# Two column chunks of an output projection computed as a pair with seven products, and a pinned eviction of the first values

## The chip, the cores and the metric

The kernel runs on one core of a Trainium2 chip (trn2). The metric is the device time of one execution in microseconds (us); three runs of the kernel before took 1334.0 to 1335.42 us, their median is 1334.83 us. One other execution was profiled; it took 1334.18 us, and 1332.5 us of it lie between its first and its last instruction (the span).

## The reference

One decoder layer on 256 rows of width 2048, all in float32, cut to what matters here:

```python
h = rmsnorm(x, g_mix)
proj = h @ w_in                                   # q, k, v of 16 heads and three gates of width 2048
...                                               # three kinds of causal attention: o_a, o_b, o_c
merged = (gates[:, :, 0] * (flat(o_a) @ w_branch[:ea])
          + gates[:, :, 1] * (flat(o_b) @ w_branch[ea:eb])
          + gates[:, :, 2] * (flat(o_c) @ w_branch[eb:]))
x = x + merged @ w_out                            # the output projection, 2048 x 2048
h2 = rmsnorm(x, g_ffn)
gu = h2 @ w_gu                                    # 2048 x 10752 (D_FF = 5376, twice)
x = x + (silu(gu[..., :D_FF]) * gu[..., D_FF:]) @ w_down
```

## The kernel before, in words

**Products.** A float32 matrix is split into a part `hi` that the matmul takes at full speed and a rest `lo`, and each product is three matmuls, `hi*hi`, `hi*lo` and `lo*hi` (L176, L177, L178). Activations stand as columns (k-tiles of 128 by 256 rows) and are the stationary operand, weights stream. A weight tile of two k-tiles by 512 columns (512 KB) is loaded by SP's queue into `w_raw` (4 buffers) or `g_raw` (6 buffers); ScalarE (ACT) casts it to `w_hi` (line 110), VectorE (DVE) subtracts to get `w_lo` (line 110); both have 5 buffers. Such a cast with its subtraction is called a split here. For both halves of the rows (t = 0, 1) one split feeds 12 matmuls of 128x512.

**Plain and paired projections.** `project` computes one column chunk of 512 with 8 splits over the 16 k-tiles, 96 matmuls. `project_pair` computes two chunks at once. For the groups of four k-tiles in `wc` (a list of groups) it forms the 2x2 blocks of rows, k and columns, and takes seven products (`form`, 6 matmuls for each split) of sums of blocks instead of eight: DVE adds weight blocks into tiles `u` (L335, L321), and the activations have sums too (`h_shi`, `h_slo`, from additions at L218 to L221). For the other k-tiles it does plain products (`rest`, 12 matmuls a split). It uses four PSUM tiles, X, Y, Z and V; with `seed` set it copies X to Y and Z to V on ACT, otherwise it takes snapshots. The stages that run so are most of the input projection and the gate-up projection; the output projection runs plainly.

**Rows to columns.** What a projection gives are rows; the next one needs columns. `turn_out` (L718, L720) copies a 128x512 tile as 16-bit halves on ACT and issues a DMA transpose from ACT's queue; `turn_in` (L725) copies it back, and ACT waits in it for the transpose to land. For the merged rows `to_m` places these steps, and the result is `m_hi`, `m_lo`. For the rows after the output projection, `keep_x1` adds the residual (DVE, L1011), squares them on ACT (L438), stores them (L1013), and `next_h` turns column chunks 0 and 1 (in rooms that are `g_raw` buffers); a multiplication by the gain (DVE, L985) follows, then the split to `h_0hi` and so on, then the sums. Chunks 2 and 3 are turned by TensorE (`next_h_now`, L1003).

**Order.** Every engine takes its instructions in program order. A scheduler orders most instructions by its own costs before the launch; those marked `keep_in_program_order` keep their place among themselves. `behind(n, step)` places a step behind the n-th split: the offsets in `to_m` and `next_h` are counted in splits.

**The output projection of before.** Column chunks 0 to 3 follow one another: 12 k-tiles of chunk 0, four of chunk 1, the last four of chunk 0, the rest of chunk 1, then chunks 2 and 3. The k-tiles of the last merged chunk are so needed late. When chunk 3 begins, `begin_pair` starts the weights of the gate-up projection.

**The first values.** `keep_v` hands the eviction of the first value tiles (L803, `v<-ps,rstd`) to the scheduler; rstd is the row norm, finished by GpSimd.

Of the kernel before, what the change touches and what calls it, by code (L numbers as in the profile page):

```python
# [57 lines left out]
def hybrid_block(ctx: ExitStack, tc: tile.TileContext, x, rel_bias, w_in, w_branch, w_out, w_gu, w_down, xT, gains,  # L58
# [29 lines left out]
    pool(ctx, "rim", "right").tile([P, (LINE - 32) // 4], F32, name="rim")  # L88
    wpool = pool(ctx, "wpool", "right", 5)
    scratch = pool(ctx, "scratch", "right", 12)  # L90
    gx = pool(pgx, "gx", "right", 2)

    def half_kb(dt=F32):
# [249 lines left out]
    def project_pair(acts, w, colA, colB, begun=None, nxt=None):  # L343
# [37 lines left out]
        add_into(u, b22)  # L381
        form(X, 6, u, False, True)
        x2 = snapshot(X)
        rest(1, ks[2], Z, V)
        if not by_dma(w, colA):
            add_into(b12, b22)
        form(X, 7, b12, False, True)
        x3 = snapshot(X)
        rest(1, ks[3], Z, V, stop=True)
        if seed:  # L390
            nc.vector.tensor_sub(x3, V, x3)
            c22 = x3
# [28 lines left out]

    p1 = pool(ph1, "p1", "left")
    o_raw = p1.tile([P, NH, S], F32, name="o_raw")
    h = Columns(p1, "h", KT)
    hs = Both(p1, h, WC)

    pa = pool(pat, "pa", "left", 2)

# [369 lines left out]
    def keep_v(g, ps):  # L798
        heads["v", g] = v = pa.tile([P, NT, NB], F32, name="v")

        def scaled():
            for t in range(NT):
                nc.scalar.activation(v[:, t, :], ps[t], AF.Copy, scale=rstd[:, t:t + 1])  # L803
            yield

        if g:
            finish_stages([scaled()])
        else:
            stages.append(scaled())
# [122 lines left out]

    pgx.close()
    m = Columns(pool(pm, "pm", "right"), "m", KT)

    LAST_H = 2

    def to_m(c, srcs, rooms, out_at, in_at):
        n = split_count[0]
        for t in range(NT):  # L940
            behind(n + out_at[t], turn_out, srcs[t], rooms[t])
            behind(n + in_at[t], lambda t: m.put(c, t, turn_in(rooms[t]), True), t)

    def take_gate(gt, src):
        gt.append(half_kb())
# [6 lines left out]
    for c in range(4):  # L952
        turning = [rooms[(NT * c + t) % len(rooms)] for t in range(NT)]
        ms = [room[:, :NB] for room in turning]
        for b, (k0, nk) in enumerate(((0, H_A), (H_A, H_B), (H_A + H_B, H_C))):
            gt = ahead_gates.pop((c, b), None) or list(kept.get((c, b), ()))
            for t in range(NT):
                if (c, b) in unopened:
                    behind(split_count[0] + 1 + t, lambda t, gt: tc.keep_in_program_order(opened(gt[t], gt[t], t)), t, gt)
                elif not gt:  # L960
                    behind(split_count[0] + 1 + t, take_gate, gt, gate_mem[b, c, t])
            if (c, b + 1) in unopened:
                ahead_gates[c, b + 1] = []
                for t in range(NT):
                    behind(split_count[0] + 1 + t, take_gate, ahead_gates[c, b + 1], gate_mem[b + 1, c, t])
            ps = project(o, k0, w_branch, k0 * P, nk, c * NB)
            for t in range(NT):
                if b == 0:
                    nc.vector.tensor_mul(ms[t], ps[t], gt[t])
                else:  # L970
                    nc.vector.tensor_mul(gt[t], ps[t], gt[t])
                    nc.vector.tensor_add(ms[t], ms[t], gt[t])
        if c == unopened[-1][0]:
            tc.keep_in_program_order(nc.scalar.preload_act_table_set("natural_log_exp_and_others"))
        to_m(c, ms, turning, *(((4, 7), (10, 12)) if c < 3 else ((4, 5), (8, 8))))


    def out_of_rows(src, rooms, pl, name, bufs):
# [8 lines left out]

    def next_h(c, xc):
        n, rooms = split_count[0], []
        out_at, in_at = ((4, 8), (11, 14)) if c < 1 else ((4, 7), (9, 11))  # L990
        for t in range(NT):
            behind(n + out_at[t], lambda t: out_of_rows(xc[t], rooms, gx, "g_raw", 6), t)
            behind(n + in_at[t], into_h, c, t, rooms)
        if c in WC:
            behind(n + in_at[1] + 1, lambda: h2.put_sums(c, *[r[:, NB:].rearrange("p (k q) -> p k q", k=4) for r in rooms]))
# [21 lines left out]
        else:  # L1017
            stages.append(next_h_now(c, xc))

    for c in range(4):  # L1020
        xc = [half_kb() for _ in range(NT)]
        for t in range(NT):
            behind(split_count[0] + (1, 2)[t], lambda t: fetch(xc[t], x[t * P:(t + 1) * P, c * NB:(c + 1) * NB]), t)
        if c == 0:
            ps = project(m, 0, w_out, 0, KT, 0, upto=12)
            second = project(m, 0, w_out, 0, KT, NB, upto=4)
            project(m, 0, w_out, 0, KT, 0, ps, 12)
        elif c == 1:
            ps = project(m, 0, w_out, 0, KT, NB, second, 4)
        else:  # L1030
            ps = project(m, 0, w_out, 0, KT, c * NB)
        if c == 0:
            ph1.close()
            pe = pool(ctx, "pe", "left")
            WD = (4, 6, 8)
            ORDER = [0, 1, 2, 4, 3, 6, 5, 8, 7, 9, 10]
            EARLY = 3
            a = Chunks(None, "a", NF // 4, WD, False)
            for e in ORDER[:EARLY]:
                a.place(pe, e)  # L1040
            h2 = Chunks(pool(h2_stack, "h2p", "left"), "h", KT // 4, WC)
            gx = pool(h2_stack, "gx2", "left", 2)
        if c == 3:
            ahead = begin_pair(h2, w_gu, 0, D_FF)
        keep_x1(c, ps, xc)
# [239 lines left out]
```

## Time and profile before

| | before |
|---|---|
| time, median of 3 runs | 1334.83 us (1334.0 to 1335.42) |
| profiled execution | 1334.18 us, span 1332.5 us |
| PE busy | 1325.1 us, 99% |
| DVE busy | 1198.2 us, 90% |
| ACT busy | 939.8 us, 71% |
| GpSimd busy | 61.8 us, 5% |
| input projection and gates | 4 to 540 us |
| branch projection | 540 to 595.4 us |
| output projection | 595.4 to 679.2 us, 384 matmuls |
| gate-up, then down projection | from 679.2 us |

Time outside the span is 1334.18 - 1332.5 = 1.7 us. In the rows of the trace that follow, the first number is the start in us from the span's begin, the second the duration; a `[... <-...]` at the end is idle time of that engine before the row, and what ended it. PE is TensorE, ACTq the queue of ScalarE that issues DMAs. A `x2` sums two rows. Durations of matmuls overlap: the pitch from start to start is what a matmul costs.

### The profile page before, as it was taken

What the parts mean: (1) busy time and instruction counts of PE and PEld (TensorE: products, weight loads), DVE (VectorE), ACT (ScalarE), POOL (GpSimd) and SP (SyncE); (2) the same over time, 40 slices, a digit from 0 to 9 for tenths busy, and PEclk for the clock granted to TensorE, in tenths of its full rate; (3) what the DMA queues carried; (4) which work ended last, traced back from release to release, by engine and by line L of the source; (5) the groups of instructions that cost most, each with busy time, mean ns of one, the idle gap of its engine ahead of it and who ended that gap; (6) DMA issues with size and microseconds to landing.
All of it is one profiled execution on the core that took longest, in us unless ns stands there. A gap on an engine that the chain in (4) does not pass through costs nothing.

```text
span 1332.5 us, 17482 instructions
## 1 busy us (share of the span) xinstructions
PE 1325.1 (99%) x6202; PEld 1152.8 (87%) x6202; DVE 1198.2 (90%) x1261; ACT 939.8 (71%) x1209; POOL 61.8 (5%) x85
## 2 busy tenths in 40 slices
PE   9999999999999999999999999999999999999998
PEld 7888888888888888888888888888888888888887
DVE  7898998999889988785899999999999998999998
ACT  7677867777677766766766778787777776664563
POOL 0300100000111000000020000000000000000000
PEclk9999999999999999999999999999999999999999
DMA  9995868767777866997996966677878887867662
GB/s 342 305 303 173 249 189 258 242 209 229 238 244 246 282 194 239 283 277 230 293 289 234 244 226 234 201 230 256 261 246 221 232 280 255 291 236 275 231 213 102
DMA packets 203623, 325.80 MB, mean 245 GB/s; under 512 B 44648, under 2 KB 55424, under 8 KB 203536
## 3 DMA queue, kind: packets, MB, share of 16 engines
q1 hardware_dynamic: 151488, 291.02, 64.3%
q0 software_dynamic: 8416, 18.44, 6.7%
q10 hardware_dynamic: 43632, 15.24, 5.8%
q8 instruction: 48, 0.79, 0.2%
q14 instruction: 39, 0.32, 0.1%
HBM read 304.18 MB, written 12.08 MB: 237 GB/s over the span
## 4 chain that ended last, share of the span: by engine, by line
PE 87%; DVE 5%; DMA 3%; issue 2%; ACT 2%; POOL 0%; SPq 0%; DVEq 0%; ACTq 0%; POOLq 0%
PE ps L177 11%; PE ps L176 11%; PE ps L178 11%; PE qs L177 10%; PE qs L176 10%; PE qs L178 10%; PE z L177 4%; PE z L178 4%; PE z L176 4%; DVE w_lo L110 3%; PE v L176 2%; PE v L177 2%; PE v L178 2%; ACT w_hi L110 1%; DMA w_raw<-in_w_down 1%
## 5 line engine op out<-in xcount | busy, mean ns | idle before, releaser
L110 DVE TENSOR_TENSOR w_lo<-w_raw,w_hi 128x1024 fp32r<-128x1024 f32 x308 | 373.8, 1219 | 64.9 <-ACT w_hi L110 63.7
L110 ACT CAST w_hi<-w_raw 128x1024 fp32r<-128x1024 f32 x308 | 319.7, 1046 | 75.5 <-PE qs L178 21.5
L110 ACT CAST w_hi<-u 128x1024 fp32r<-128x1024 f32 x156 | 163.2, 1047 | 166.0 <-DVE u L321 87.5
L110 DVE TENSOR_TENSOR w_lo<-g_raw,w_hi 128x1024 fp32r<-128x1024 f32 x208 | 248.0, 1218 | 19.2 <-ACT w_hi L110 17.9
L110 ACT CAST w_hi<-g_raw 128x1024 fp32r<-128x1024 f32 x208 | 214.1, 1048 | 67.8 <-PE ps L178 15.4
L110 DVE TENSOR_TENSOR w_lo<-u,w_hi 128x1024 fp32r<-128x1024 f32 x156 | 186.9, 1219 | 22.0 <-ACT w_hi L110 21.6
L177 PE MATMUL ps<-w_lo,h_hi 128*128 128x512 f32 x328 | 125.0, 381 | 0.5 <-DVE w_lo L110 0.5
L178 PE MATMUL ps<-w_hi,h_lo 128*128 128x512 f32 x328 | 124.3, 379 | 0.0
L177 PE MATMUL qs<-w_lo,h_hi 128*128 128x512 f32 x316 | 120.6, 382 | 0.0
L178 PE MATMUL qs<-w_hi,h_lo 128*128 128x512 f32 x316 | 119.8, 379 | 0.0
L176 PE MATMUL ps<-w_hi,h_hi 128*128 128x512 f32 x328 | 118.6, 381 | 0.1
L176 PE MATMUL qs<-w_hi,h_hi 128*128 128x512 f32 x316 | 114.4, 382 | 0.0
L321 DVE TENSOR_TENSOR u<-u,g_raw 128x1024 f32<-128x1024 f32 x88 | 103.9, 1216 | 0.0
L177 PEld LDWEIGHTS ps<-w_lo,h_hi 128*128 128x128 f32 x328 | 62.0, 189 | 9.5 <-DVE w_lo L110 0.9
L176 PEld LDWEIGHTS ps<-w_hi,h_hi 128*128 128x128 f32 x328 | 61.7, 189 | 9.5 <-ACT w_hi L110 0.7
L178 PEld LDWEIGHTS ps<-w_hi,h_lo 128*128 128x128 f32 x328 | 62.0, 189 | 8.6
L178 PEld LDWEIGHTS qs<-w_hi,h_lo 128*128 128x128 f32 x316 | 59.7, 189 | 8.3
L176 PEld LDWEIGHTS qs<-w_hi,h_hi 128*128 128x128 f32 x316 | 59.5, 189 | 8.5 <-issue 0.4
L177 PEld LDWEIGHTS qs<-w_lo,h_hi 128*128 128x128 f32 x316 | 59.8, 189 | 8.1
L335 DVE TENSOR_TENSOR u<-g_raw 128x1024 f32<-128x1024 f32 x44 | 53.5, 1216 | 1.0 <-DMA g_raw<-in_w_gu 1.0
L176 PE MATMUL v<-w_hi,h_hi 128*128 128x512 f32 x112 | 43.1, 385 | 0.0
L177 PE MATMUL v<-w_lo,h_hi 128*128 128x512 f32 x112 | 42.6, 380 | 0.0
(426 smaller groups left out, 2947.6 us busy)
## 6 DMA issues: line engine op xcount, KB each, us to landing
w_raw<-in_w_in SPq DMA_DIRECT2D x100, 512.0 KB, 5.7
g_raw<-in_w_in SPq DMA_DIRECT2D x88, 512.0 KB, 5.7
g_raw<-in_w_gu SPq DMA_DIRECT2D x88, 512.0 KB, 5.8
w_raw<-in_w_gu SPq DMA_DIRECT2D x88, 512.0 KB, 5.9
w_raw<-in_w_down SPq DMA_DIRECT2D x56, 512.0 KB, 5.1
w_raw<-in_w_branch SPq DMA_DIRECT2D x32, 512.0 KB, 5.2
w_raw<-in_w_out SPq DMA_DIRECT2D x32, 512.0 KB, 5.9
g_raw<-in_w_down SPq DMA_DIRECT2D x32, 512.0 KB, 5.5
```

Source lines behind the costliest of these rows:

```text
L110: for op in nc.scalar.copy(hi, src), nc.vector.tensor_sub(lo, src, hi.bitcast(F32)):
L176: nc.tensor.matmul(ps, ah, wh, start=start, stop=False, **how)
L177: nc.tensor.matmul(ps, ah, wl, start=False, stop=False, **how)
L178: nc.tensor.matmul(ps, al, wh, start=False, stop=stop, **how)
L321: tc.keep_in_program_order(nc.vector.tensor_add(d, d, a))
L335: nc.vector.tensor_add(d, a, b)
```

## The change

1. Chunks 0 and 1 of the output projection run as one `project_pair` with `wc=(0,)`: the first four k-tiles by the seven products, the other twelve plainly, seeded. 19 splits take the place of 16. Its first splits (`begin_pair`) stand ahead of the end of the branch projection. The merged rows of chunk 0 get their sums (`m_sums`); `rest` stands in two loops in the middle.
2. The residual rows of both chunks are loaded together, and `keep_x1` for both comes after the whole pair; `next_h` for chunk 0 gets offsets (1,3),(6,8) in place of (4,8),(11,14). `to_m` for chunk 3 gets (3,4) in place of (4,5).
3. `h` and `hs` move to a pool on the other side of memory, which is freed before the pair's tiles are made.
4. The evictions in `keep_v` are pinned in program order, and the first ones wait until the paired stages have begun.

```diff
+    ph = pool(pgx, "ph", "right")
...
-        rest(1, ks[2], Z, V)
+        middle = ks[2:1 + len(ks) // 2]
+        for k in middle:
+            rest(1, k, Z, V)
...
-        rest(1, ks[3], Z, V, stop=True)
+        for k in ks[2 + len(middle):]:
+            rest(1, k, Z, V, stop=k == ks[-1])
...
         def scaled():
+            while not in_pairs[0]:
+                yield
             for t in range(NT):
-                nc.scalar.activation(v[:, t, :], ps[t], AF.Copy, scale=rstd[:, t:t + 1])
+                tc.keep_in_program_order(nc.scalar.activation(v[:, t, :], ps[t], AF.Copy, scale=rstd[:, t:t + 1]))
...
+    m_sums = Both(pool(pair_stack, "ms", "right"), m, (0,))
+    gx = pool(pair_stack, "gx3", "right", 2)
...
+        if c in m_sums.wc:
+            behind(n + in_at[1] + 1, lambda: m_sums.put_sums(c, *words))
...
+            if (c, b) == (3, 2):
+                ahead = begin_pair(m_sums, w_out, 0, NB, True)
...
-        to_m(c, ms, turning, *(((4, 7), (10, 12)) if c < 3 else ((4, 5), (8, 8))))
+        to_m(c, ms, turning, *(((4, 7), (10, 12)) if c < 3 else ((3, 4), (8, 8))))
...
-        out_at, in_at = ((4, 8), (11, 14)) if c < 1 else ((4, 7), (9, 11))
+        out_at, in_at = ((1, 3), (6, 8)) if c < 1 else ((4, 7), (9, 11))
...
-    for c in range(4):
...
-        if c == 0:
-            ps = project(m, 0, w_out, 0, KT, 0, upto=12)
-            second = project(m, 0, w_out, 0, KT, NB, upto=4)
-            project(m, 0, w_out, 0, KT, 0, ps, 12)
-        elif c == 1:
-            ps = project(m, 0, w_out, 0, KT, NB, second, 4)
-        else:
-            ps = project(m, 0, w_out, 0, KT, c * NB)
...
+    xc = take_x((0, 1), 6)
+    ps, _ = project_pair(m_sums, w_out, 0, NB, ahead)
...
+    for c in range(2):
+        keep_x1(c, ps[NT * c:NT * (c + 1)], xc[c])
+    for c in range(2, 4):
+        xc, = take_x((c,), 1)
+        ps = project(m, 0, w_out, 0, KT, c * NB)
```

What the change does to the order shows at three places. Line numbers shift by a few: L110 is L111 after, L438 is L442, L718, L720 and L725 are L722, L724 and L729, L803 is L809, L985 is L1002, L1011 is L1028, L1013 is L1030.

ScalarE near 40 us, at the end of the first values, before:

```order
L110 CAST w_hi_540<-w_raw_538 128x1024
L803 ACTIVATE v_459<-ps_137,rstd_108 128x512
L803 ACTIVATE v_459<-ps_138,rstd_108 128x512
L110 CAST w_hi_564<-g_raw_556 128x1024
L110 CAST b_shi1_102<-o_raw_97 128x1024
L110 CAST w_hi_568<-g_raw_558 128x1024
L110 CAST w_hi_582<-g_raw_578 128x1024
```

and after:

```order
L111 CAST w_hi_541<-w_raw_539 128x1024
L111 CAST w_hi_565<-g_raw_557 128x1024
L111 CAST b_shi1_105<-o_raw_100 128x1024
L111 CAST w_hi_569<-g_raw_559 128x1024
L809 ACTIVATE v_462<-ps_140,rstd_111 128x512
L809 ACTIVATE v_462<-ps_141,rstd_111 128x512
L111 CAST w_hi_585<-g_raw_581 128x1024
```

Three casts (the first two of the next weights and one of activation sums) moved ahead of the two evictions.

ScalarE at the start of the output projection, where the last merged chunk is turned (`o_raw` is the memory of its rooms), before:

```order
L718 COPY o_raw_97<-o_raw_97 128x1024
L110 CAST w_hi_5641<-w_raw_5639 128x1024
L718 COPY o_raw_97<-o_raw_97 128x1024
L720 DMA_TRANSPOSE o_raw_97<-o_raw_97 128x8x128
L110 CAST w_hi_5661<-w_raw_5659 128x1024
L720 DMA_TRANSPOSE o_raw_97<-o_raw_97 128x8x128
L110 CAST w_hi_5679<-w_raw_5677 128x1024
L725 COPY o_raw_97<-o_raw_97 128x2x512
L110 CAST m_hi_4825<-o_raw_97 128x4x128
```

and after, where `qs_5576` is X, `qs_5577` is Y, `z_5578` is Z and `v_5579` is V of the pair:

```order
L369 COPY qs_5577<-qs_5576 128x512
L722 COPY o_raw_100<-o_raw_100 128x1024
L371 COPY v_5579<-z_5578 128x512
L724 DMA_TRANSPOSE o_raw_100<-o_raw_100 128x8x128
L111 CAST w_hi_5648<-u_5556 128x1024
L722 COPY o_raw_100<-o_raw_100 128x1024
L111 CAST w_hi_5664<-w_raw_5662 128x1024
L111 CAST w_hi_5682<-w_raw_5680 128x1024
L724 DMA_TRANSPOSE o_raw_100<-o_raw_100 128x8x128
L317 COPY sc_5660<-qs_5576 128x512
```

The seed copy of Z to V stands behind the first copy of the merged rows, and casts and a snapshot stand between the transposes and the copies back.

ScalarE behind the end of chunk 0, before, from the first transpose of its new rows to the first copy back:

```order
L720 DMA_TRANSPOSE g_raw_5841<-g_raw_5841 128x8x128
L110 CAST w_hi_5905<-w_raw_5903 128x1024
L110 CAST w_hi_5924<-w_raw_5922 128x1024
L718 COPY g_raw_5928<-sc_5534 128x1024
L720 DMA_TRANSPOSE g_raw_5928<-g_raw_5928 128x8x128
L110 CAST w_hi_5946<-w_raw_5944 128x1024
L1013 DMA x1_93<-sc_5534 128x512
L110 CAST w_hi_5965<-w_raw_5963 128x1024
L110 CAST w_hi_5986<-w_raw_5984 128x1024
L725 COPY g_raw_5841<-g_raw_5841 128x2x512
```

and after, behind the end of the pair (`sc_5572` to `sc_5574` are rows of both chunks):

```order
L722 COPY g_raw_5947<-sc_5572 128x1024
L722 COPY g_raw_5988<-sc_5573 128x1024
L722 COPY g_raw_6009<-sc_5574 128x1024
L111 CAST w_hi_6044<-w_raw_6042 128x1024
L1030 DMA x1_96<-sc_5572 128x512
L724 DMA_TRANSPOSE g_raw_5947<-g_raw_5947 128x8x128
L724 DMA_TRANSPOSE g_raw_5988<-g_raw_5988 128x8x128
L724 DMA_TRANSPOSE g_raw_6009<-g_raw_6009 128x8x128
L729 COPY g_raw_5947<-g_raw_5947 128x2x512
L111 CAST w_hi_6068<-w_raw_6066 128x1024
L722 COPY g_raw_6072<-sc_5575 128x1024
L111 CAST w_hi_6089<-w_raw_6087 128x1024
```

Five casts stood between the first transpose and the copy that waits for it; now three transposes stand in a row and the copy back follows at once. VectorE has the last of the four gain rows, and what follows it, before:

```order
L985 TENSOR_TENSOR g_raw_5969<-g_raw_5969,par_73 128x512
L110 TENSOR_TENSOR h_slo0_5753<-g_raw_5841,h_shi0_5752 128x4x128
L1011 TENSOR_TENSOR sc_5899<-qs_5901,sc_5899 128x512
L110 TENSOR_TENSOR w_lo_6172<-w_raw_6169,w_hi_6171 128x1024
L1011 TENSOR_TENSOR sc_5900<-qs_5902,sc_5900 128x512
```

and after:

```order
L111 TENSOR_TENSOR w_lo_6240<-w_raw_6237,w_hi_6239 128x1024
L111 TENSOR_TENSOR h_slo0_5907<-g_raw_5988,h_shi0_5906 128x4x128
L219 TENSOR_TENSOR g_raw_6072<-g_raw_6072 128x256
L1002 TENSOR_TENSOR g_raw_6009<-g_raw_6009,par_73 128x512
L222 TENSOR_TENSOR g_raw_5947<-g_raw_5947 128x256
L111 TENSOR_TENSOR w_lo_6258<-w_raw_6255,w_hi_6257 128x1024
L220 TENSOR_TENSOR g_raw_6072<-g_raw_6009,g_raw_6072 128x256
L1020 TENSOR_TENSOR sc_6170<-tr_6165,par_73 128x512
L111 TENSOR_TENSOR w_lo_6277<-w_raw_6274,w_hi_6276 128x1024
```

Before, the last gain row stood ahead of the new rows of chunk 2 (L1011, `sc_5899`); it now stands behind them (L1028 in the numbers of after) and ahead of the first rows of chunk 2 that TensorE turned (L1020).

More of the change, by code (lines that the diff above doesn't have):

```diff
@@ L423, in hybrid_block @@
     o_raw = p1.tile([P, NH, S], F32, name="o_raw")
-    h = Columns(p1, "h", KT)
-    hs = Both(p1, h, WC)
+    h = Columns(ph, "h", KT)
+    hs = Both(ph, h, WC)
     pa = pool(pat, "pa", "left", 2)
@@ L934, in hybrid_block, with into_m @@
     m = Columns(pool(pm, "pm", "right"), "m", KT)
+    pair_stack = ExitStack()
+    m_sums = Both(pool(pair_stack, "ms", "right"), m, (0,))
+    gx = pool(pair_stack, "gx3", "right", 2)
     LAST_H = 2
+    def into_m(c, t, room, words):
+        words.append(turn_in(room))
+        m.put(c, t, words[-1], True)
     def to_m(c, srcs, rooms, out_at, in_at):
-        n = split_count[0]
+        n, words = split_count[0], []
         for t in range(NT):
             behind(n + out_at[t], turn_out, srcs[t], rooms[t])
-            behind(n + in_at[t], lambda t: m.put(c, t, turn_in(rooms[t]), True), t)
+            behind(n + in_at[t], into_m, c, t, rooms[t], words)
+        if c in m_sums.wc:
+            behind(n + in_at[1] + 1, lambda: m_sums.put_sums(c, *words))
     def take_gate(gt, src):
@@ L1018, in keep_x1, with take_x @@
             stages.append(next_h_now(c, xc))
-    for c in range(4):
-        xc = [half_kb() for _ in range(NT)]
-        for t in range(NT):
-            behind(split_count[0] + (1, 2)[t], lambda t: fetch(xc[t], x[t * P:(t + 1) * P, c * NB:(c + 1) * NB]), t)
-        if c == 0:
-            ps = project(m, 0, w_out, 0, KT, 0, upto=12)
-            second = project(m, 0, w_out, 0, KT, NB, upto=4)
-            project(m, 0, w_out, 0, KT, 0, ps, 12)
-        elif c == 1:
-            ps = project(m, 0, w_out, 0, KT, NB, second, 4)
-        else:
-            ps = project(m, 0, w_out, 0, KT, c * NB)
[L1032 to L1042, printed above, removed]
+    def take_x(cs, at):
+        xc = [[half_kb() for _ in range(NT)] for c in cs]
+        for i, c in enumerate(cs):
+            for t in range(NT):
+                behind(split_count[0] + at + NT * i + t,
+                       lambda i, c, t: fetch(xc[i][t], x[t * P:(t + 1) * P, c * NB:(c + 1) * NB]), i, c, t)
+        return xc
+    xc = take_x((0, 1), 6)
+    ps, _ = project_pair(m_sums, w_out, 0, NB, ahead)
+    pair_stack.close()
+    ph1.close()
+    pe = pool(ctx, "pe", "left")
+    WD = (4, 6, 8)
+    ORDER = [0, 1, 2, 4, 3, 6, 5, 8, 7, 9, 10]
+    EARLY = 3
+    a = Chunks(None, "a", NF // 4, WD, False)
+    for e in ORDER[:EARLY]:
+        a.place(pe, e)
+    h2 = Chunks(pool(h2_stack, "h2p", "left"), "h", KT // 4, WC)
+    gx = pool(h2_stack, "gx2", "left", 2)
+    for c in range(2):
[3 more added lines that the diff above has]
+        ps = project(m, 0, w_out, 0, KT, c * NB)
         if c == 3:
```

## The prediction

> **What bounds the kernel now.** I read the busy shares first, then the windows around the changed stage, then what TensorE (PE) waits for, and last the timelines of ACT and DVE at the places where the change puts other instructions.
>
> ```profile
> span 1332.5 us, 17482 instructions
> PE 1325.1 (99%) x6202; PEld 1152.8 (87%) x6202; DVE 1198.2 (90%) x1261; ACT 939.8 (71%) x1209; POOL 61.8 (5%) x85
> ...
> L177 PE MATMUL ps<-w_lo,h_hi 128*128 128x512 f32 x328 | 125.0, 381 | 0.5 <-DVE w_lo L110 0.5
> ```
>
> PE leaves 1332.5 - 1325.1 = 7.4 us of the span. The reader should see two bounds in that: no change in the order alone can gain more than some 7 us, and whatever PE waits for that it did not wait for before is paid in full. The next engine is DVE, and how close it is depends on the stage:
>
> ```profile
> core 0: us, PE busy (x) PEld busy (x) DVE busy (x) ACT busy (x) POOL busy (x), PEclk, DMA share, GB/s
> 500.00:600.00 100.00, 100.00 (x465) 87.57 (x464) 79.55 (x92) 67.38 (x71) 0.00 (x0) 1.00 0.88 267
> 600.00:650.00 50.00, 50.00 (x233) 43.78 (x232) 29.73 (x30) 34.37 (x43) 0.00 (x0) 1.00 0.90 268
> 650.00:700.00 50.00, 50.00 (x241) 43.82 (x240) 46.59 (x58) 35.72 (x49) 7.82 (x11) 1.00 0.86 273
> 700.00:800.00 100.00, 100.00 (x465) 87.44 (x464) 95.86 (x92) 71.34 (x80) 0.00 (x0) 1.00 0.75 234
> 800.00:900.00 100.00, 99.97 (x462) 86.59 (x461) 97.19 (x92) 77.81 (x88) 0.00 (x0) 1.00 0.70 223
> ```
>
> In the output projection's first part DVE has 40% to spare, in its second 7%, and in the gate-up stage behind it 3 to 4%. So DVE enters the gate-up stage with whatever lead it has, and cannot win back a lost one there: a delay at 680 us reaches the end of the kernel. PE's waits as such are tiny:
>
> ```profile
> PE ps L177 <- DVE w_lo L110: 0.7, 2, 0.5
> PE z L177 <- DVE w_lo L110: 0.5, 1, 0.5
> ```
>
> **The six matmuls.** The two chunks took 2 x 96 = 192 matmuls; the pair takes 7 products x 6 + 12 rests x 12 = 186. The pitch is 100 us / 465 = 0.215 us (first window), though a row shows 0.38. PE is never idle in this stage, so they lie on the path: -1.29 us.
>
> The Trainium skill, "TensorE: Matmul & The Clock Gate", section "Back-to-back issue gap", gives about 131 ns as the sustained pitch of a 512-column matmul in a stream with weight loads, and 216 ns for one alone. By the first figure the six would save 0.79 us; this trace shows the second in a full stream, so -1.29 stays.
>
> **The pinned first values.** Here PE's longest hole in the stage is visible:
>
> ```profile
> 42.72 1.27 ACT L803 ACTIVATE v<-ps,rstd 128x512 f32<-128x512 f32 x2 [2.18 <-POOL rstd L192]
> ...
> 44.95 1.22 DVE L110 TENSOR_TENSOR w_lo<-g_raw,w_hi 128x1024 fp32r<-128x1024 f32 x1 [3.15 <-ACT w_hi L110]
> ...
> 51.50 0.38 PE L176 MATMUL ps<-w_hi,h_hi 128*128 128x512 f32 x1
> 52.36 0.48 PE L177 MATMUL ps<-w_lo,h_hi 128*128 128x512 f32 x1 [0.48 <-DVE w_lo L110]
> ```
>
> ACT waits 2.18 us for rstd with casts queued behind it, DVE waits 3.15 us for the cast, and PE comes to a w_lo that is late: 52.36 - 51.50 = 0.86 against a pitch of 0.215, a hole of 0.65 us. After, three casts stand ahead of the evictions, and the 2.18 us are filled. I take the whole hole, -0.65 us. The bounds: 0, if the next split is late instead, to -0.65. The later evictions of values (inside the paired stages) are pinned too, so one may hold a PSUM tile longer; in the order it sits behind two copies that PE's transposes release, and the tile is wanted about a microsecond after. I take 0 for it, with a bound of +1.5 (two evictions by 0.64, from the row of 1.27 x2).
>
> **Inside the pair.** DVE gets four weight additions and three more subtractions of 128x1024, 7 x 1.22 = 8.5 us by the 44.95 row, and some smaller sums; in 600 to 650 it was idle 50 - 29.7 = 20 us, and I cost them at 0 under that cover; if the cover is gone, up to 8.5 us of w_lo work is late. ACT gets three casts and some copies, with 15.6 us idle in the same window: 0 by amount. SP loads the same 32 tiles, only in another order: 0. By order ACT is not at 0:
>
> ```profile
> 52.23 0.58 ACT L316 COPY sc<-ps 128x512 f32<-128x512 f32 x1
> ...
> 599.05 1.04 ACT L718 COPY o_raw<-o_raw 128x1024 uint16<-128x1024 uint16 x1 [0.83 <-DVE o_raw L972]
> ...
> 602.02 1.25 ACTq L720 DMA_TRANSPOSE o_raw<-o_raw  x1
> ...
> 606.11 1.34 ACT L725 COPY o_raw<-o_raw 128x1024 uint16<-128x1024 uint16 x1 [1.70 <-DMA o_raw<-o_raw]
> ...
> 609.82 1.35 ACT L725 COPY o_raw<-o_raw 128x1024 uint16<-128x1024 uint16 x1 [1.72 <-DMA o_raw<-o_raw]
> ...
> 611.98 0.61 ACT L110 CAST m_hi<-o_raw 128x512 fp32r<-128x512 f32 x1
> 612.50 2.94 ACT L110 CAST w_hi<-w_raw 128x1024 fp32r<-128x1024 f32 x3
> ...
> 621.30 0.38 PE L176 MATMUL ps<-w_hi,m_hi 128*128 128x512 f32 x1
> ```
>
> The merged rows of the last chunk come at 599.05, 3.6 us after the branch projection's end; their first copy (1.04) now stands ahead of the copy of Z to V (0.58), so V would be ready 3.6 + 0.95 + 0.6 = 5.1 us into the pair; in the new order one weight subtraction of DVE that stood ahead of these rows is gone from there (about 1 us), so 4.2. PE wants it after three forms of 1.29 us, at 3.9: a wait of 0.3 to 0.4. Two issues (602.02) with 1.25 us each follow. Then the last merged columns: before, their cast ended at 612.6 and PE used them first at 621.30, 8.7 us to spare. The pair has no such detour by chunk 1 and wants them about 7 us earlier, and a snapshot now stands ahead of the copy back: I expect two waits of some 0.25 us. Sum of the pair's own waits: +0.9 us, the nearest rows being the 0.5 us waits above. Bounds: 0, and 3, the time between the two copies back (609.82 - 606.11 = 3.7) less what I have counted, if the second transpose is late in full.
>
> **Behind the pair.** This is the large term. Both chunks' residual rows now come at the pair's end, E, where before chunk 0's came 13.5 us ahead of chunk 1's (623.23 and 636.68, L1011). What follows on ACT is priced by these rows:
>
> ```profile
> g_raw<-in_w_gu SPq DMA_DIRECT2D x88, 512.0 KB, 5.8
> ...
> o_raw<-o_raw ACTq DMA_TRANSPOSE x6, 7.9
> g_raw<-g_raw ACTq DMA_TRANSPOSE x6, 6.2
> ...
> 623.23 1.28 DVE L1011 TENSOR_TENSOR sc<-qs,sc 128x512 f32<-128x512 f32 x2
> ...
> 623.94 0.63 ACT L438 ACTIVATE sc<-sc 128x512 f32<-128x512 f32 x1 [0.63 <-DVE sc L1011]
> ...
> 624.58 1.03 ACT L718 COPY g_raw<-sc 128x1024 uint16<-128x1024 uint16 x1
> ...
> 636.68 1.28 DVE L1011 TENSOR_TENSOR sc<-ps,sc 128x512 f32<-128x512 f32 x2
> ...
> 640.40 0.33 ACTq L1013 DMA_DIRECT2D x<-sc  x1
> ...
> 644.86 1.25 ACTq L720 DMA_TRANSPOSE g_raw<-g_raw  x1
> ...
> 646.20 1.05 ACT L110 CAST w_hi<-w_raw 128x1024 fp32r<-128x1024 f32 x1 [1.37 <-issue]
> ...
> 656.66 0.69 DVE L985 TENSOR_TENSOR g_raw<-g_raw,par 128x512 f32<-128x512 f32 x1 [0.44 <-ACT g_raw L725]
> ...
> 671.70 2.47 DVE L335 TENSOR_TENSOR u<-g_raw 128x1024 f32<-128x1024 f32 x2 [0.99 <-DMA g_raw<-in_w_gu]
> 674.08 3.49 DVE L110 TENSOR_TENSOR w_lo<-g_raw,w_hi 128x1024 fp32r<-128x1024 f32 x3
> ...
> 682.65 1.23 DVE L110 TENSOR_TENSOR w_lo<-u,w_hi 128x1024 fp32r<-128x1024 f32 x1 [0.77 <-ACT w_hi L110]
> ...
> 686.64 0.46 PE L177 MATMUL z<-w_lo,h_shi 128*128 128x512 f32 x1
> ```
>
> A DMA transpose holds ACT for 1.25 us while it issues (the cast at 646.20 waited 1.37 for "issue"). From E: additions 1.2, four squares 4 x 0.64 (624.58 - 623.94), three copies and a cast 4 x 0.95 (the pitch (2.94 - 1.04) / 2 of the casts at 612.50), a store 0.33: the first transpose issues at E + 7.8, and three of them hold ACT to E + 11.5. The first lands after 6.2 (median of six), at E + 14.0; ACT sits in the copy back until then, where before five casts stood between the two. The copy costs 1.2 (from 609.82 to the next row). Three casts, a copy, the second copy back, a small cast and two stores (6.2 us) come before the fourth transpose: E + 21.5, landed E + 27.7, copied by E + 29. Two casts, two small casts and a store (3.05) stand before the last copy back (1.2): the last gain row on DVE comes at about E + 33. Before, it came at 656.66 - 636.68 = E + 20.
>
> From that row to the subtraction of the second `u` split of the gate-up weights, the new order has 26 DVE instructions: 11 of 128x1024 at a pitch of 1.135 (row 674.08: (3.49 - 1.22) / 2), 11 of 128x512 at 0.60 (row 636.68: 1.28 - 0.68), 4 of 128x256 at an estimated 0.33, half of that and a little: 20.4 us, ending at E + 53.5. The gate-up weights also wait for rooms: `g_raw` buffers hold the turned rows until DVE's sums are made, then 5.8 us of load and 1 of cast follow. Two such rooms come free 5.5 and 4.3 us of DVE work ahead of the row that needs the new weights: 6.85 - 5.5 and 6.85 - 4.3 less the 1.4 already waited make 1.4 + 1.1 = 2.5 us, or 0 if loads come sooner; the 0.99 at 671.70 is such a wait. PE wants that split after the 192 matmuls of chunks 2 and 3 (41.4), 24 of the gate-up stage (5.2), eight small transposes (0.9) and 7 matmuls (1.5): E + 49.0. Late by 4.5 to 7.0; I take 6.0. Before, the split ended at 683.9 and was used at 686.64, 2.7 us to spare, so this stage held no stall. The lower bound is 0 (the first rival), the upper 7.0 + 2 x 1.7 = 10.4 (the 7.9 of the merged rows' transposes in place of 6.2, in the two rounds that are in series).
>
> **Sum.** -1.29 - 0.65 + 0.9 + 6.0 = +5.0 us on the profiled execution's 1334.18, that is 1339.2. The median of the runs stands 0.65 above that execution, so 1339.8; I say 1340.
>
> **Rivals.**
> - *The rows are hidden anyway.* The lead decides it: DVE may run up to five splits ahead (five `w_lo` buffers), and the wait for E + 14 gives it time to. Had it 4 splits in hand at E + 33 that stand behind this row in the order, 4 x 1.135 = 4.5 us of the 20.4 would be done, and the split is in time. For it: DVE idles 20 us of 600 to 650. Against it: the order is fixed, and the rows of the list stand behind the gain row. It turns at a lateness under 0.5 us; then -1.94 + 0.9 = -1.0, or 1333.8, no slower than before.
> - *Everything in time and the small holes gone.* Also without the pair's waits: -1.94, and up to 0.8 from waits like those of 0.5 above that shift: 1334.83 - 2.7 = 1332.1. Against it: three events must coincide.
> - *The transposes queue behind each other.* Three issue in 3.75 us. If each lands only after the one before (two issued 1.9 us apart in the merged rows were copied back 3.7 apart, 606.11 and 609.82), the last row comes 3 to 5 us later still: 1343 to 1346.
> - *A cold PE.* The granted clock is 1.00 in every window above because PE never stops. A single wait as long as 6 us would be the first of its length; if the clock then halved for as long as the wait lasted, PE would do 3 us of work in those 6, and 3 us are added: 1343. More likely the wait is in five pieces of 1 to 2 us, one at each split. The Trainium skill, "TensorE: Matmul & The Clock Gate", section "HAM oscillation - how this bites in real kernels", warns of idle gaps over about 3.4 us; no run here shows one yet.
>
> **Chances.** Late rows near the sum 0.50, transposes queueing 0.10, cold clock 0.04, hidden 0.28, all gone 0.08. The changes within 0.2% of before (2.7 us, about what a measurement of this kernel can tell from no change) are the hidden rows: 0.28. Faster 0.08, slower 0.64. The likeliest case alone spans 1336 to 1344 (lateness 2 to 10); the range reaches down to the hidden rows, 1333, and up to the queueing transposes, 1346.
>
> **What would show it.** After, PE should have a new group of waits on `w_lo` (L111) near 680 us, in `ps` and `z` rows, of 4 to 7 us in all; ACT a long wait in the copy back (L729) on the transpose some 8 to 14 us behind the pair's end; DVE its last gain row (L1002) about 33 us behind that end; the 0.48 wait at 52 us should be gone. If PE shows no wait at 680 us, the lead was larger than my walk has it, and the prediction is wrong there; if the waits sit in the pair (V, m_hi), its +0.9 was too small.

## The result, and the profile after

The changed kernel is slower: its four runs took 1341.71 to 1349.9 us, median 1344.55, against a median of 1334.65 us before (four runs, 1334.0 to 1335.42). The ratio is 1.008, with a 95% interval of 1.0061 to 1.0099. The profiled execution took 1342.05 us, 7.9 us more than that of before; the rest of the 9.9 us between the medians differs from execution to execution, and is taken up below.

The page of the changed kernel, its first lines:

```profile
span 1340.3 us, 17488 instructions
PE 1328.1 (99%) x6196; PEld 1152.4 (86%) x6196; DVE 1209.8 (90%) x1276; ACT 946.3 (71%) x1218; POOL 63.5 (5%) x85
```

The six matmuls are gone (6202 to 6196) and the share of PE still reads 99%. What PE waits for tells more. Columns: engine, tile and line, what released it, us in total, times, longest:

```profile
PE ps L177 <- ACT w_hi L111: 2.6, 1, 2.6
PE qs L177 <- ACT qs L369: 1.6, 1, 1.6
PE tr L422 <- PEq L1286: 0.8, 1, 0.8
PE ps L178 <- DVE w_lo L111: 0.8, 1, 0.8
PE v L177 <- ACT v L371: 0.5, 1, 0.5
```

The `tr` wait was there before. The other four are new, two in the pair (L369, L371) and two at the start of the gate-up stage. By the starts of PE's rows, before and after:

| stage on PE | before | after | difference |
|---|---|---|---|
| up to the end of the branch projection | 595.40 | 595.08 | -0.3 |
| chunks 0 and 1 of the output projection | to 636.84: 41.4 | to 638.53: 43.4 | +2.0 |
| chunks 2 and 3 | to 679.16: 42.3 | to 681.31: 42.8 | +0.5 |
| gate-up, up to the first V product | to 687.80: 8.6 | to 695.57: 14.3 | +5.6 |
| the rest of the span | 644.7 | 644.7 | 0.0 |

The sum is +7.8 us, the difference of the spans. The pair should have saved 1.3 and cost 2.0, so 3.3 us are lost inside it. The rows of the two largest holes, ScalarE first, then PE, from the timeline of the changed kernel:

```profile
577.79 1.26 ACTq L724 DMA_TRANSPOSE o_raw<-o_raw  x1
...
581.76 4.13 ACTq L724 DMA_TRANSPOSE o_raw<-o_raw  x1
...
592.16 1.35 ACT L729 COPY o_raw<-o_raw 128x1024 uint16<-128x1024 uint16 x1 [3.28 <-DMA o_raw<-o_raw]
...
595.98 1.36 ACT L729 COPY o_raw<-o_raw 128x1024 uint16<-128x1024 uint16 x1
597.37 0.62 ACT L111 CAST m_hi<-o_raw 128x512 fp32r<-128x512 f32 x1
597.89 1.04 ACT L111 CAST w_hi<-w_raw 128x1024 fp32r<-128x1024 f32 x1
598.84 0.58 ACT L369 COPY qs<-qs 128x512 f32<-128x512 f32 x1
...
597.45 0.38 PE L179 MATMUL z<-w_hi,b_slo 128*128 128x512 f32 x1
599.47 0.48 PE L177 MATMUL qs<-w_hi,m_hi 128*128 128x512 f32 x1 [1.64 <-ACT qs L369]
...
601.52 0.48 PE L177 MATMUL v<-w_hi,m_hi 128*128 128x512 f32 x1 [0.48 <-ACT v L371]
```

Read it backwards. PE's second product waits at 599.47 for Y, the copy of X (L369), which starts at 598.84 only. Ahead of it in ScalarE's queue stand the two copies back of merged chunk 2 (592.16 and 595.98), with casts of columns and weights. In the first of them ScalarE waits 3.28 us: its DMA transpose was issued at 577.79 and landed 14.3 us later. The transpose of the second was issued at 581.76 and landed 14.2 us later, at 595.96, just as ScalarE came to it. The two transposes of this chunk took 4.8 and 11.1 us before. V then comes 0.65 us late as well. The holes are 2.02 - 0.22 = 1.8 us and 0.65 us (start to start, less the pitch). Most of the rest of the 3.3 us are holes of 0.1 to 0.2 us: two right behind these, and six from 615.9 to 618.5 us, 0.6 us in all, where the last merged columns are first used.

Behind the pair, ScalarE, VectorE and PE of the changed kernel:

```profile
644.24 1.34 ACTq L724 DMA_TRANSPOSE g_raw<-g_raw  x1
...
650.93 1.35 ACT L729 COPY g_raw<-g_raw 128x1024 uint16<-128x1024 uint16 x1 [3.88 <-DMA g_raw<-g_raw]
...
667.97 0.69 DVE L1002 TENSOR_TENSOR g_raw<-g_raw,par 128x512 f32<-128x512 f32 x1
...
678.33 1.22 DVE L111 TENSOR_TENSOR w_lo<-g_raw,w_hi 128x1024 fp32r<-128x1024 f32 x1
...
681.27 1.05 ACT L111 CAST w_hi<-g_raw 128x1024 fp32r<-128x1024 f32 x1 [5.92 <-DMA g_raw<-in_w_gu]
...
686.89 1.04 ACT L111 CAST w_hi<-g_raw 128x1024 fp32r<-128x1024 f32 x1 [4.05 <-DMA g_raw<-in_w_gu]
...
687.97 1.22 DVE L111 TENSOR_TENSOR w_lo<-g_raw,w_hi 128x1024 fp32r<-128x1024 f32 x1 [3.79 <-ACT w_hi L111]
...
690.31 2.44 DVE L111 TENSOR_TENSOR w_lo<-u,w_hi 128x1024 fp32r<-128x1024 f32 x2
...
687.99 0.48 PE L177 MATMUL ps<-w_hi,h_0hi 128*128 128x512 f32 x1 [2.63 <-ACT w_hi L111]
689.25 0.48 PE L178 MATMUL ps<-w_lo,h_0hi 128*128 128x512 f32 x1 [0.78 <-DVE w_lo L111]
...
692.99 0.63 PE L179 MATMUL z<-w_hi,h_slo 128*128 128x512 f32 x1
693.41 0.60 PE L177 MATMUL z<-w_hi,h_shi 128*128 128x512 f32 x1
```

The last gain row comes at 667.97, the weights of the gate-up stage behind it. ScalarE waits 4.05 us for the sixth `g_raw` load of that stage; it was issued at 679.57, right behind the subtraction at 678.33, which read the buffer that it fills, and landed at 686.80. PE waits 2.63 us for the cast, then 0.78 for its `w_lo`; VectorE stands idle 3.79 us for the same cast. The last two rows show something else: a pitch of 0.42 us, twice 0.215. The granted clock tells why:

```profile
650.00:675.00 25.00, 24.86 (x119) 21.46 (x118) 21.57 (x31) 23.00 (x30) 0.00 (x0) 1.00 0.97 307
675.00:700.00 25.00, 21.47 (x93) 17.75 (x93) 20.27 (x24) 12.09 (x20) 7.25 (x9) 0.93 0.93 273
700.00:725.00 25.00, 25.00 (x117) 21.91 (x116) 24.57 (x25) 17.88 (x20) 0.39 (x2) 1.00 0.70 243
```

In 675 to 700 us the clock is 0.93 of full speed. It falls behind the two waits; that they cause it is tried below (the filled wait). In the 5.6 us of this stage, 2.8 + 1.04 = 3.8 are waits; most of the 1.8 left is the slower pitch. VectorE runs at 98% (24.57 of 25) behind it, and nothing is won back: the rest of the span is as long as before.

### The profile page after: what moved, and what is told of

It reads as the page before. It is cut to its first block, busy times and chain, and to the rows that moved or that the text cites. A ratio compares the mean times of both kernels' runs of the same rounds, so it can differ in the third digit from the quotient of the medians.

```text
span 1340.3 us, 17488 instructions
## 1 busy us (share of the span) xinstructions
PE 1328.1 (99%) x6196; PEld 1152.4 (86%) x6196; DVE 1209.8 (90%) x1276; ACT 946.3 (71%) x1218; POOL 63.5 (5%) x85
## 4 chain that ended last, share of the span: by engine, by line
PE 89%; DMA 4%; DVE 3%; ACT 2%; issue 2%; SPq 0%; ACTq 0%; DVEq 0%
PE ps L178 11%; PE ps L177 11%; PE ps L179 11%; PE qs L177 10%; PE qs L178 10%; PE qs L179 10%; PE z L178 4%; PE z L179 4%; PE z L177 4%; PE v L177 3%; PE v L178 3%; PE v L179 3%; DVE w_lo L111 1%; PE tr L178 1%; PE tr L177 1%
## 5 line engine op out<-in xcount | busy, mean ns | idle before, releaser
L111 DVE TENSOR_TENSOR w_lo<-w_raw,w_hi 128x1024 fp32r<-128x1024 f32 x304 | 369.4, 1221 | 48.8 <-ACT w_hi L111 47.6
L111 ACT CAST w_hi<-w_raw 128x1024 fp32r<-128x1024 f32 x304 | 315.3, 1047 | 61.8 <-PE ps L179 15.4
L111 ACT CAST w_hi<-u 128x1024 fp32r<-128x1024 f32 x159 | 166.1, 1048 | 168.0 <-DVE u L322 90.3
L111 DVE TENSOR_TENSOR w_lo<-g_raw,w_hi 128x1024 fp32r<-128x1024 f32 x212 | 253.2, 1221 | 22.3 <-ACT w_hi L111 21.0
L111 ACT CAST w_hi<-g_raw 128x1024 fp32r<-128x1024 f32 x212 | 218.7, 1049 | 75.3 <-PE ps L179 15.0
L111 DVE TENSOR_TENSOR w_lo<-u,w_hi 128x1024 fp32r<-128x1024 f32 x159 | 191.0, 1221 | 22.4 <-ACT w_hi L111 21.9
L178 PE MATMUL ps<-w_lo,h_hi 128*128 128x512 f32 x344 | 131.1, 381 | 0.0
L179 PE MATMUL ps<-w_hi,h_lo 128*128 128x512 f32 x344 | 130.4, 379 | 0.0
L177 PE MATMUL ps<-w_hi,h_hi 128*128 128x512 f32 x344 | 124.0, 381 | 0.1
L178 PE MATMUL qs<-w_lo,h_hi 128*128 128x512 f32 x300 | 114.7, 382 | 0.0
L179 PE MATMUL qs<-w_hi,h_lo 128*128 128x512 f32 x300 | 113.8, 379 | 0.0
L177 PE MATMUL qs<-w_hi,h_hi 128*128 128x512 f32 x300 | 109.3, 382 | 0.2 <-ACT sc L317 0.2
```

The lines of the kernel that those rows point to most:

```text
L111: for op in nc.scalar.copy(hi, src), nc.vector.tensor_sub(lo, src, hi.bitcast(F32)):
L177: nc.tensor.matmul(ps, ah, wh, start=start, stop=False, **how)
L178: nc.tensor.matmul(ps, ah, wl, start=False, stop=False, **how)
L179: nc.tensor.matmul(ps, al, wh, start=False, stop=stop, **how)
```

## The experiments

**The pin alone.** The kernel before, with the edit of `keep_v` only:

```diff
         def scaled():
+            while not in_pairs[0]:
+                yield
             for t in range(NT):
-                nc.scalar.activation(...)
+                tc.keep_in_program_order(nc.scalar.activation(...))
```

> The kernel before with the pinned evictions of the values alone; the output projection stays plain. If the hole at 51.5 us (0.65 us) is closed and no other opens, the time falls by 0.3 to 0.7 us, 1334.0 to 1334.4 against 1334.65. If the pin holds a PSUM tile in the paired stages, as the bound of +1.5 had it, it is 1335 to 1336. Either way the pair is then answerable for all of the 7 to 10 us that the change costs.

Median 1334.52 us of 11 runs against 1334.37 of 15, ratio 1.000 (0.9991 to 1.0008). In the trace the hole at 51.5 us is gone and the span is 1332.0 against 1332.5, but a new one of 0.3 us stands at 312 us. The gain, if there is one, lies under what the runs resolve; a cost does not show either.

**The pair without the pin.** The same edit taken back in the changed kernel.

> The changed kernel with the evictions of the values left to the scheduler, as before. If the pair alone costs the time, it is 0.3 to 0.7 us slower than the changed kernel in a run with the same clock: 1342.4 to 1343 at best, with the same waits of 2.4 us in the pair and 3 to 4 us at the start of the gate-up stage. If the pin has a part in it, it is more than 1 us faster than the changed kernel.

Median 1345.73 us (1342.37 to 1347.86), ratio 1.008 (1.006 to 1.01), as with the pin. The pair alone is the cause. This kernel's profiled execution was one of the long ones (span 1346.2), and shows what those are made of:

```profile
PE qs L177 <- ACT qs L369: 3.7, 1, 3.7
PE ps L177 <- ACT w_hi L111: 3.6, 1, 3.6
```

```profile
600.00:625.00 25.00, 23.02 (x91) 18.97 (x92) 17.28 (x19) 17.80 (x21) 0.00 (x0) 0.86 0.57 178
...
685.00:700.00 15.00, 10.90 (x41) 8.59 (x40) 9.26 (x12) 8.47 (x14) 1.38 (x2) 0.77 1.03 295
```

Both waits are longer, and behind each the clock (the third number from the right) falls further, to 0.86 and 0.77.

**Seven rooms.** One more `g_raw` buffer behind the pair (line numbers two higher):

```diff
+    g_bufs = [6]
-        raw = pl.tile([P, 2, NB], F32, name="g_raw", bufs=6 if pl is gx else 4) if pl else ...
+        raw = pl.tile([P, 2, NB], F32, name="g_raw", bufs=g_bufs[0] if pl is gx else 4) if pl else ...
...
     gx = pool(h2_stack, "gx2", "left", 2)
+    g_bufs[0] = 7
```

> The changed kernel with seven g_raw buffers instead of six behind the pair, so that the turned rows and the first weights of the gate-up stage share one room more. Theory of rooms (the sixth gate-up load is issued only at 679.57 us because its buffer is that of the first one, and lands at 686.8): the load goes out about 4 to 8 us earlier, the ScalarE wait of 4.05 us and the TensorE wait of 2.63 us are gone, at most 1 us of waits is left at the start of the gate-up stage, the clock stays at 1.000 and the time is 1336 to 1338. Theory of VectorE (26 instructions behind the last gain row end too late whatever the loads do): VectorE's queue ends its second u split as late as now less 3.8 us at most, TensorE still waits 2 to 4 us there, spread over several splits, and the time is 1339 to 1342.

Median 1339.94 us (1339.18 to 1341.07), ratio 1.004 (1.0026 to 1.0054). PE's waits from 675 to 700 us:

```profile
PE ps L178 <- DVE w_lo L111: 0.8, 1, 0.8
PE ps L177 <- ACT w_hi L111: 0.7, 1, 0.7
PE z L178 <- DVE w_lo L111: 0.2, 1, 0.2
```

The 2.6 us wait is gone (the 0.7 us for `w_hi` is at a later split, 695 us), the clock stays at 1.00, and the four runs lie within 1.9 us. So the room was what the late weights waited for. By the starts of PE's rows the gate-up stage, up to the first V product, takes 11.2 us, against 14.3 in the changed kernel and 8.6 before. What is left, 1.7 us, lies between the two theories, and the time (1336 to 1338 expected of the rooms) shows that the rooms are not the whole cost: the pair's own waits are the same here, 2.0 us.

**A filled wait.** Twelve matmuls of constants ahead of the third split of the gate-up stage:

```diff
+            if w is w_gu:
+                idle(12)
             form(Y, 2, second, True, False, True)
```

> The changed kernel with 12 matmuls of constants (128x512, 2.6 us) on TensorE between the second and the third split of the gate-up stage, where it waits; nothing reads their result. Theory of the cold clock (the wait of 2.6 us lets the granted clock fall to half, which costs 1.7 us in the profiled run and 4 to 8 in the slower ones): the matmuls fill the wait, the granted clock stays at 1.000, no matmul behind it has a pitch of 0.42, and the time is 1339.5 to 1341 in every run, although 2.6 us of work were added. Theory without the clock (the slower runs come from loads that land late): the time is 1342 to 1350 as now, with the same spread, or 2 us more.

Half of the expectation failed. In the profiled execution (span 1340.0, against 1340.3 without the 2.6 us of matmuls) the clock is 1.00 from 685 to 700 us, as the cold clock has it: with the wait filled, the clock does not fall. But the runs took 1341.72 to 1349.1 us, with clocks of 1.0 down to 0.997: the spread is not from this wait alone. The mean clock in the runs of the changed kernel bears that out: 0.998 in the one of 1341.71, 0.995 in the one of 1349.9, which is 0.003 x 1348 = 4 us of the 8.2 between them. The run of 1347.06 has 0.997: by the same estimate 1.3 us of its 5.4. So the clock has a quarter to a half of the spread here, with an error of some 0.7 us on each clock from its rounding; that the rest is longer waits is not shown.

**The copy back behind the seeds.** In `to_m`, chunk 2 only:

```diff
-... ((4, 7), (10, 12)) if c < 3 else ...
+... ((4, 7), (10, 12 + 2 * (c == 2))) if c < 3 else ...
```

> The changed kernel with the second copy back of merged chunk 2 placed two splits later, so that on ScalarE it stands behind the two seed copies instead of ahead of them; nothing else is moved. Theory of the copy back (the seed copy of X to Y waits in ScalarE's queue behind a copy back whose transpose lands 14 us after its issue, and TensorE waits 1.6 us in a quick run and 3.7 in a slow one for it): the waits on L369 and L371 fall from 2.1 to 0.5 us or less, the time by 1.5 to 2 us at equal waits behind the pair, and the slowest runs come down by more, so 1340 to 1346. Theory of the seeds themselves (they are late because the first forms are, whatever stands ahead): the waits stay above 1.5 us.

Median 1344.3 us (1342.7 to 1344.69), ratio 1.0072 (1.0058 to 1.0085). The wait on Y is gone, as the theory of the copy back says, and the four runs lie within 2 us. But the waits on the seeds did not fall to 0.5 us, since the wait on V grew, and the median is no lower, since the waits in the pair moved:

```profile
PE v L177 <- ACT v L371: 1.8, 1, 1.8
PE z L177 <- ACT m_hi L111: 1.2, 1, 1.2
```

**Chunk 1 by TensorE.** `next_h_now` in place of `next_h` for chunk 1 (`LAST_H = 1`), with the sums put behind it.

> The changed kernel with the new rows of chunk 1 turned to columns by TensorE (as those of chunks 2 and 3 are) instead of by DMA: eight more small transposes on TensorE (0.9 us), two copies, two DMA transposes and two copies back less on ScalarE, two g_raw rooms less in use. Theory of the turned rows (two chunks' rows turned at once behind the pair hold ScalarE, VectorE and the rooms): the waits at the start of the gate-up stage fall from 3.6 us to at most 1 us, the clock stays at 1.000, the time is 1336.5 to 1339 with a spread under 3 us. Theory of the loads alone (the gate-up weights land late because ten loads are issued in a burst): the waits stay at 2 to 4 us and the time at 1341 to 1346.

Median 1338.95 us (1337.29 to 1341.24), ratio 1.0035 (1.0021 to 1.0049): the lowest median of a single edit to the changed kernel, though its interval overlaps that of the seven rooms. From 675 to 700 us PE waits once:

```profile
PE ps L177 <- ACT w_hi L111: 0.8, 1, 0.8
```

This although the profiled execution had the longer wait on Y (3.3 us, with a clock of 0.93 behind it), and eight more transposes stand on PE. The gate-up stage, up to the first V product, takes 8.65 us, as before (8.64); the pair takes 46.9, against 41.4 for the plain chunks. The theory of the turned rows holds; that of the loads alone falls. Turning chunk 1 on TensorE takes work from ScalarE and VectorE and frees two rooms at once, so this run does not part the rooms from the rest.

**The three together.** Copy back, chunk 1, seven rooms.

> The changed kernel with the copy back behind the seeds, chunk 1 turned by TensorE, and seven rooms. If the waits found are the whole cost, what is left is the saving of 1.9 us less 0.9 us of transposes and less some 0.5 to 1 us of waits for V: 1333.5 to 1335.5, no different from before. If the pair has a further cost (DMA that runs late in the whole stage), it is 1336 to 1339.

Median 1341.64 us (1338.22 to 1343.03), ratio 1.0048 (1.0036 to 1.0061), outside of what either reading expected, and no better than chunk 1 by TensorE alone (the two intervals overlap). The profiled execution has the two moved waits of the copy back (1.8 and 1.2 us), 0.4 us on Y and 0.5 us at 695 us. Why its median lies above that execution's 1339.54 is not shown.

**The old offsets.** `next_h` for chunk 0 with (4,8),(11,14) again.

> The changed kernel with the old offsets of next_h for chunk 0, (4,8),(11,14), so that the copies, transposes and copies back of chunk 0's new rows stand 3 to 6 splits (8 to 15 us) further back. Theory of the turned rows (their arrival sets the start of the gate-up stage): the last gain row comes 5 to 10 us later, the waits at 685 us grow from 3.6 to 8 us or more, the time is 1347 to 1355. Theory of the burst (three transposes at once behind the pair are what is slow): with the steps spread out each transpose lands sooner, ScalarE is free meanwhile, and the time is 1338 to 1344.

Median 1344.95 us (1340.35 to 1347.29), ratio 1.0072 (1.0052 to 1.0092): the same as with the new ones, and a miss for both theories. The waits at the gate-up start are spread over more places (2.7 us in three for `w_hi`, 1.0 for new rows), and with 1.1 us more for other weights their sum is 4.8 us, against 3.4. The offsets, which were a part of the change, do not move the median beyond its interval.

**No seeds.** `begin_pair(m_sums, w_out, 0, NB)` without the last `True`.

> The changed kernel with the pair of the output projection unseeded: X and Z are copied to snapshots, Y and V start from nothing, and VectorE adds the parts at the end (one subtraction and three additions of 128x512 more or less in its place). No matmul of TensorE waits for a copy on ScalarE any more. Theory of the seed copies: the waits on L369 and L371 (2.1 us in the changed kernel, 3.3 to 4 in the others) are gone and nothing of their size takes their place before the pair's end; the time is 1339 to 1343, and the runs are closer together. Theory of the whole ScalarE queue (casts of weights and merged columns stand behind the same copy back, and TensorE waits for them instead): waits of 1.5 us or more on w_hi or m_hi between 595 and 620 us, and the time is 1342 to 1346.

Median 1342.49 us (1340.93 to 1343.83), ratio 1.0061 (1.0045 to 1.0076). No wait on a seed is left; in the pair there are

```profile
PE v L178 <- DVE w_lo L111: 1.5, 1, 1.5
PE v L177 <- ACT m_hi L111: 0.3, 1, 0.3
```

The 1.5 us are the second theory's wait, on `w_lo` where it named `w_hi` or `m_hi`: the casts stand behind the same copies back as the seeds did. The time lies in the part that both expected. The gate-up start waits 4.1 us in this execution.

**No seeds, chunk 1 by TensorE.**

> The unseeded pair, with the new rows of chunk 1 turned by TensorE as well. If the seed copies and the turned rows are the two causes and nothing else is, the saving of the six matmuls and of the pin (1.9 us) is left less 0.9 us for the transposes and 1 us of small waits: 1333.5 to 1335.5. If other waits take their place, 1336 to 1340.

Median 1337.07 us (11 runs, 1334.35 to 1340.17) against 1334.1, ratio 1.0024 (1.0015 to 1.0033): in the range of the second reading, other waits in their place, and the lowest median of the pairs, still slower than the plain projection. PE's waits from 590 to 700 us:

```profile
PE v L178 <- DVE w_lo L111: 1.2, 1, 1.2
PE v L177 <- ACT m_hi L111: 0.3, 1, 0.3
```

The profiled execution's span is 1334.6, 2.1 us more than before. Its gate-up stage takes 8.65 us, as before; the pair takes 44.0 against 41.4, so all that is left is lost inside the pair. The two waits are 1.5 us of it; the rest are short holes that no run takes apart. None of the versions beats the kernel before.

**The loads held.** The first three `g_raw` loads of the pair, and SP's queue behind them, wait for the second product of the last merged chunk, by a GpSimd copy into each buffer:

```diff
+        if after is not None:
+            tc.keep_in_program_order(nc.gpsimd.tensor_copy(raw[:, 0, 0:8], after))
...
+                held["by"] = ms[1][:, 0:8]
                 ahead = begin_pair(m_sums, w_out, 0, NB, True)
```

> The changed kernel in which the first three g_raw loads of the pair are held until the second product of the last merged chunk is added (about 588 us instead of 575), by a copy of eight columns on GpSimd into each buffer ahead of its load; SP's queue behind them waits with them, so the burst of eight 512 KB loads at 574 to 580 us is gone while the two transposes of merged chunk 2 are under way. Theory of the burst (the transposes land 14 us after their issue because the loads share the DMA engines): they land in 5 to 8 us, as in the kernel before (4.8 and 11.1) and with the pin alone (5.0 and 6.8), and ScalarE's copies back wait for nothing. The loads are late instead, so TensorE may wait 1 to 4 us at 595 us and the time need not fall: 1340 to 1347. Theory that the transposes are slow for another reason (their place or their rooms): they still take 13 us or more.

This tells why the transposes of merged chunk 2 land late. DMA issues from 576 to 590 us, with the median time to landing as the last number, in the changed kernel,

```profile
w_raw<-in_w_out SPq DMA_DIRECT2D x4, 512.0 KB, 10.2
g_raw<-in_w_out SPq DMA_DIRECT2D x2, 512.0 KB, 11.6
o_raw<-o_raw ACTq DMA_TRANSPOSE x2, 14.3
```

with the pin alone,

```profile
w_raw<-in_w_out SPq DMA_DIRECT2D x5, 512.0 KB, 5.6
o_raw<-o_raw ACTq DMA_TRANSPOSE x2, 5.9
```

and with the loads held:

```profile
o_raw<-o_raw ACTq DMA_TRANSPOSE x2, 3.3
```

The loads are the cause: with none issued beside them the transposes land in 3.3 us, even below the 5 to 8 expected, and the copies back wait for nothing. The kernel is slower for it (median 1349.19 us, ratio 1.0112, 1.0088 to 1.0136), beyond the 1340 to 1347 expected, since the held loads are now late: PE's waits in the pair are 4.7 us, against 2.1.

**Held, no seeds, chunk 1 by TensorE.**

> The unseeded pair with chunk 1 turned by TensorE, as in the kernel that came to 1337, with the same three loads held. If the slow transposes are behind its waits of 1.2 us on w_lo and behind its spread of 5.8 us, the waits between 595 and 620 us go under 1 us in all, the time is 1334 to 1336 and the spread under 3 us. If the held loads are themselves late, TensorE waits 1 to 4 us near 595 us, and the time is 1337 to 1341.

Median 1341.26 us (1340.32 to 1341.76), ratio 1.0048 (1.0032 to 1.0064), just above the second reading's range: the held loads are late, with holes on PE of 1.2, 1.0 and 1.5 us between 595 and 601, and a clock of 0.90 in 600 to 625 us. The six runs lie within 1.4 us. Whether quick transposes alone would end the 1.2 us wait stays open, since the late loads take its place.

## Why the prediction was right, and where not

The direction, the place and the order of size came out: slower, with the loss at the gate-up start and in the pair, 1344.55 in a range of 1333 to 1346. By the medians the loss is 9.9 us where 1340 meant some 5, and 1344.55 lies above the likeliest case (1336 to 1344), in the part of the range that was kept for transposes that queue behind the pair, which is not what happened. That much is luck. Its working against the profiled execution, which it was made for: +5.0 was forecast, +7.9 measured.

- *Six matmuls, -1.29.* The count fell by six and the pitch is unchanged. Agreed, and swallowed.
- *The pin, -0.65.* The hole at 51.5 us closed, PE is 0.3 us ahead at 595 us. Alone the pin moves the median by +0.15 us, inside its interval of about 1.2 us to either side.
- *Inside the pair, +0.9 forecast, 3.3 measured, over the bound of 3.* This is the term that was mis-sized. V was foreseen 0.3 to 0.4 late (0.65 measured), the last merged columns 0.5 in two waits (0.6 in six small holes). Missed was Y, 1.8 us: I walked ScalarE's queue only from the last merged chunk's rows on, and did not look at what stands ahead of L369 there, the copies back of the chunk before. And I took landing times of transposes from before, though the change puts eight loads beside these, by SP's queue, whose order I had costed at 0.
- *Behind the pair, +6.0 forecast, 5.6 to 6.1 measured* (gate-up start alone 5.6, chunks 2 and 3 another 0.5). The size is right, the parts are not, so the agreement is in part luck. ScalarE was quicker than the walk: the first transpose at 644.24 is 5.7 us behind the pair's end (638.53) where I had 7.8, the last gain row 29.4 where I had 33. The second `u` split ended 54.2 us behind it, inside of the 53.5 to 56, but 3.8 us of that VectorE stood idle for the cast of the late load (687.97). Without that wait it would have ended near 50.4, 1.4 us behind the 49.0 at which PE wants it and not 4.5 (an estimate; no run shows it alone). I called VectorE's 26 instructions the cause and the rooms a supplement of 0 to 2.5 us; seven rooms take half of PE's 3.4 us of waits away, the whole of the largest. And the holes behind the waits are 3.8 us; most of the rest is the clock, for which I had a rival of its own with a chance of 0.04.
- *A cold PE.* It happened, and costs some 1.7 us here and more in the longer runs. I expected the wait in pieces under the length that matters; one piece was 2.6 us, with one of 0.8 right behind it, and that is enough. The Trainium skill, "TensorE: Matmul & The Clock Gate", section "HAM oscillation — how this bites in real kernels", names gaps over about 3.4 us; here, in windows of 25 us, the clock falls with waits of 2.6 us (0.93), 3.3 (0.93) and 3.7 (0.86), and stays at 1.00 in the windows with waits of 1.6 and 2.1; one execution has 0.97 and then 0.96 around a wait of 2.0. In this kernel less than the page's gap is enough. Nor does the longest single wait decide: with the loads held and no seeds, two waits of 1.0 and 0.8 us, 1.3 us apart, were followed by a pitch of 0.43 from 598.5 us on, while in the filled wait's kernel one of 2.1 us by itself was not.
- *The rows are hidden, the transposes queue.* The first did not occur. The second did not as I had it: behind the pair the transposes landed in 4.5 to 7.7 us. The second of them held ScalarE 3.78 us while it issued, but the copy back behind had to wait for the first one's landing anyway (650.93). Transposes did land late, but ahead of the pair.

Not settled is why the executions of the pair kernels differ by up to 8 us. In the changed kernel the clock has a quarter to a half of it, in the unseeded pair with chunk 1 by TensorE nothing that shows (1334.35 and 1340.17 us, both at a clock of 1.0). The waits differ too (1.6 to 3.7 us on the same copy of Y), and what makes one execution's transposes land later than another's was not shown.

## What to carry to other kernels

Saving work on the busiest engine is worth its count only if every hand-over around it stays in time: here 1.3 us of matmuls saved made four waits of 5.5 us in all and a slower clock behind them. Two of the waits come from loads that the pair brings forward, beside transposes that ScalarE's queue stands behind; two come from chunks that now end at one moment, so that all that follows from them (squares, turns, rooms, weights) must be done in the time that one chunk had. When a step is moved, read on each in-order queue what stands ahead of the moved instruction as well as behind it, and price the DMAs that it waits for by the load that the change itself puts beside them. A buffer that serves two purposes ties their deadlines together: one more room took away the largest wait.

## What the runs showed of the hardware that was not expected

- A DMA transpose of a 128x1024 tile of 16-bit words landed in 3.0 and 3.5 us with no weight load issued beside it (the loads held), mostly in 4.5 to 10 with some, and in 14.2 and 14.3 with eight loads of 512 KB issued from 572.7 to 580.9 us; the last six of these took 8 to 12 us themselves.
- A transpose's issue held ScalarE's queue 1.25 us as a rule, but 4.13 us (581.76) in that burst, with the transpose before it still under way. A transpose under way is not enough for that: in the kernel before, the issue at 602.02 held 1.25 us, while the transpose issued at 600.13 landed 6.0 us after its issue.
- Waits of 2.6 and 0.8 us on TensorE, 1.3 us apart, are followed by matmuls at a pitch of 0.42 instead of 0.215 us; so is a wait of 3.3 us by itself.
